# A two-block transformer kernel: small transfers change their queue, and two 8 KB slots join the weight ring

## The chip, the cores and the metric

One core of one Trainium2 chip. The metric is device time in microseconds of one execution, lower is better; each median is over several runs.

## What is computed

Two transformer blocks on 256 tokens of width 1024, in float32. Cut to what matters here:

```python
def first_block(x, ...):
    proj = modulate(rms_norm(x, g1), shift1, scale1) @ w_in   # width 5120
    o_sb, o_mb = stick_breaking_attention(...), moba_attention(..., rel_bias)
    x = x + gate1 * (merge(o_sb, o_mb) @ w_out)
    h2 = modulate(rms_norm(x, g2), shift2, scale2)
    # 64 experts, D=1024 -> 256 -> 1024; each token takes the best 8 of 4 groups of experts
    x = x + gate2 * (sum_e weight[t, e] * swiglu(h2, gate_e, up_e, down_e) + swiglu(h2, shared))
    return rms_norm(x, final_g)

def second_block(x, mem, ...):
    x = x + mix(short_conv, latent_attention) @ w_mix_out
    x = x + memory_cross_attention(x, mem)
    x = x + expert_choice_moe(x)          # 16 experts, D=1024 -> 1024 -> 1024; each takes its best 32 tokens
    return rms_norm(x, g)
```

The kernel reads every expert's weights once: 3 MiB for each of the 64, 12 MiB for each of the 16.

## The kernel before

**Weights.** Every weight comes in pieces of 128 x 2048 float32, 1 MiB, 8 KB on each partition. `load(src)` takes the next slot of a ring of such slots (`lanes`, a deque of slot numbers), issues the transfer on SyncE (L104) and returns the tile. The ring is changed by hand along the program: `add_lanes` appends slots that some other tile has given up, `drop_lanes` takes them back, `next_lanes` puts one at the front. It begins with ten slots (L293), five of which leave at L390. A load waits until the last reader of its slot is done. SyncE issues in order, so a load that waits holds up those behind it.

**Stages.** First the memory's keys (`memk`), the modulation (`ada`), the projections and the two attentions of block one, mostly as three float32r passes (`SP.feat`, L220) after a split of the weights on ScalarE and VectorE (L213, L214). Then routing (L755 to L898), then the first mixture, then block two's convolution, attention and memory attention, then the second mixture (L1600 to L1661).

**First mixture.** `layout` and the routing sort the experts by their number of tokens, and `_group_pairs` packs the order into 28 groups of 1, 2 or 4 experts, which share the 128 rows of a tile: eight groups of two, then four times (4, 1, 2, 2), then 4, 2, 4, 2. The first NF = 2 places are held by experts 0 and 1 whatever the routing says: `first_c` and `first_r` add 1000 x (NF - e) to their counts. So their six pieces are loaded ahead of the routing (`fixed`, L655), and group 0 uses them. All others wait for the sorted list `idx`: `Group.load` reads an expert's number into a register and issues its pieces (`eload`, L908): the halves of gate and up first, then down.

TensorE's order is written out by hand (L1055 to L1111): for each group `gate_up` (L999), parts of the `combine` of the group before (L1032, L1033) and of the `gather` for the next (L935, L936), filling work from `pieces()` (the memory's values L709, the shared expert L685 and L725), then `down` (L1023). `nxt.load()` stands at the start of each group, so one group's weights are requested while the group before is computed. Ring during this stage: eight slots at first; slots 2 and 10 join when the values are done, 11 and 7 after the shared expert's up half, 16 at its end. Slot 15 is lent for one load of group 1 (L1054, L1071).

**Order on the other engines** is made by a scheduler from the program order and its own estimates of time; only TensorE in the first mixture is fixed.

**Second mixture.** Per expert eight gate/up pieces (L1565) and four down pieces (L1634), all through `load` on SyncE; the ring has 16 slots there (17 after L1577).

**Small transfers.** Thirteen transfers are issued by GpSimd: `t5` (tables of the relative bias, L352), its product `rel` to DRAM (L358) and back as the skewed `relU` (L360), the router's weights, bias and limits (L399 to L403), three of six 1 MiB pieces that `park` brings for the filling work (L649; the other three are SyncE's), `wov` to DRAM (L898, read only by the branch for experts with too many tokens, L1116), the rotary tables (L1195, L1197) and the second router's weights (L1455). GpSimd's transfers need an area of SBUF for their descriptors.

Of the kernel before, what the change touches and what calls it, by code (L numbers as in the profile page):

```python
# [21 lines left out]
P = 128  # L22
# [8 lines left out]


N_EXP = 64
NF, N1, N2 = 2, 4, 34
CAP1, CAP2, CAP4 = 128, 64, 32


def _group_pairs():
    s = [(NF + i, 1) for i in range(N1)]
    p = [(0, NF)] + [(NF + N1 + 2 * i, 2) for i in range(N2 // 2)]  # L40
    q = [(NF + N1 + N2 + 4 * i, 4) for i in range((N_EXP - NF - N1 - N2) // 4)]
    out = []
    while s or p or q:
        g = []
        for lst in (p, p) if len(out) < 4 or not q or (len(out) % 2 and len(p) - 2 >= len(q) - len(s)) else (q, s or p):
            if lst:
                g.append(lst.pop(0))
        if g:
            out.append(g)
    return out  # L50
# [4 lines left out]
def body(tc, I, out):  # L55
    nc = tc.nc
# [34 lines left out]
    def add_lanes(*ids):  # L91
        lanes.extend(ids)

    def next_lanes(*ids):
        lanes.extendleft(reversed(ids))

    def drop_lanes(*ids):
        for i in ids:
            lanes.remove(i)

    def load(src):
        w = ring_tile()
        w = w[:, :src.shape[-1]]
        nc.sync.dma_start(w, src)  # L104
        return w
# [50 lines left out]
    def token_sums(acc):  # L156

        ps = bank("t")
        for b in range(2):
            nc.tensor.matmul(ps[:, b:b + 1], acc[:, b * P:(b + 1) * P], ones[:, :1], start=True, stop=True)  # L160
        return ps[:, :2]
# [128 lines left out]
    pa = b1.enter_context(tc.tile_pool(name="pa", bufs=1))  # L290
    open_banks(b1, "b1", d=2, s=3, t=2, a=1)
    SP = Split(14, 15, 16)
    add_lanes(17, 18, 19, 20, 21, 5, 6, 10, 12, 13)  # L293

# [15 lines left out]
    def ada_cols(ps, pair0, n):  # L312
        row = pa.tile([P, 512], F32, name="ada_row", tag="t512", bufs=3)
        nc.vector.tensor_copy(row, ps)
        pc = bank("t").rearrange("p (a u) -> p a u", a=4)
        for a in range(4):
            nc.tensor.matmul(pc[:, a, :n], row[:, a * P:(a + 1) * P], ident32[:, :n], start=True, stop=True)
        flat_mod = mod.rearrange("p g k -> p (g k)")[:, 4 * pair0:4 * (pair0 + n)]
        nc.vector.tensor_add(flat_mod.rearrange("p (u a) -> p a u", a=4), pc[:, :, :n],
                             col("b_ada", 48)[:, 4 * pair0:4 * (pair0 + n)].rearrange("p (u a) -> p a u", a=4))  # L320
# [8 lines left out]
    def memk(i):  # L329
        SP.feat(None, hm_hi, hm_lo, 256, KD,  # L330
                lambda j, ps: nc.vector.tensor_mul(mem_k[:, 2 * i:2 * i + 2], ps,
                                                   rm[:, None, :].to_broadcast([P, 2, T])), loaded=wk[i])
# [11 lines left out]
    for k in range(KD):  # L344
# [4 lines left out]
    nc.gpsimd.affine_select(out=flip, in_=flip, pattern=[[1, P]], base=1 - P, channel_multiplier=1,  # L349
                            compare_op=ALU.is_equal, fill=0.0)  # L350
    t5 = big(9, [32, 776], F32, "t5")
    nc.gpsimd.dma_start(t5, I["t5"])  # L352
    ps_r = bank("t")
    nc.tensor.matmul(ps_r[:8, :384], t5[:, :8], t5[:, 8:392], start=True, stop=True)
    rel = pa.tile([8, 384], F32, name="rel", tag="t512", bufs=3)
    nc.vector.tensor_add(rel, ps_r[:8, :384], t5[:8, 392:])
    rel_d = dram.tile([8, 384], F32, name="rel_d")
    nc.gpsimd.dma_start(rel_d, rel)  # L358
    relU = big(3, [P, 8, 256], F32, "relU")
    nc.gpsimd.dma_start(relU, bass.AP(tensor=rel_d.tensor, offset=rel_d.offset,  # L360
                                      ap=[[1, P], [384, 8], [1, 256]]))
    memk(0)
    r1 = rstd_of(pa, xT, KD, D)
    xr = big(7, [P, KD, T], F32, "xr")
# [3 lines left out]
    for i in range(4):  # L368
        mm = ada(ps_a, i, i == 0, i == 3, i)
        if i < 3:  # L370
            wk.append(load(I["w_mem_kv"][i + 1]))
            if i < 2:
                memk(i + 1)
    ada_cols(ps_a, 0, 4)
    memk(2)
    memk(3)
# [19 lines left out]
    nc.gpsimd.tensor_mul(fgfg, fg, fg)  # L396

    wr = pa.tile([P, KD, 64], F32, name="wr")
    nc.gpsimd.dma_start(wr, I["w_router"])  # L399
    rbias = const.tile([P, 64], F32, name="rbias")  # L400
    nc.gpsimd.dma_start(rbias, I["router_bias"].to_broadcast([P, 64]))
    caprow = const.tile([1, 64], F32, name="caprow")
    nc.gpsimd.dma_start(caprow, I["caprow"])  # L403


    qk = {}
# [235 lines left out]
    extra = deque([I["w_mem_kv"][4 + c] for c in range(4)] + [I["w_up_sh"], I["w_down_sh"]])  # L642
    parked = deque()

    def park(eng=nc.gpsimd):
        if extra:
            w = big(wide[0], [P, 2048], F32, "wx")
            wide.rotate(-1)
            eng.dma_start(w, extra.popleft())  # L649
            parked.append(w)  # L650

    for _ in range(2):
        park(nc.sync)
    shg = load(I["w_gate_sh"])
    fixed = [load(I["w_gu"][e, u]) for u in range(2) for e in range(NF)] + [load(I["w_down_e"][e]) for e in range(NF)]  # L655
    park(nc.sync)
    r2 = rsqrt_of(pa, token_sums(acc), D, sig_last[0])
    r2c = const.tile([P, 2], F32, name="r2c")
    nc.gpsimd.tensor_copy(r2c, r2)
# [235 lines left out]
    wov = selT  # L895
    nc.vector.scalar_tensor_tensor(wov, rkT, capc, wT, op0=ALU.is_ge, op1=ALU.mult)
    wov_d = dram.tile([64, T], F32, name="wov_d")
    nc.gpsimd.dma_start(wov_d, wov)  # L898


    xgs, yys = deque((3, 4)), deque((14, 15))
# [37 lines left out]
    class Group:  # L939
# [8 lines left out]

        def load(self):
            self.regs, self.gu, self.wd = [], [], []  # L950
            if self.i0 == 0:
                self.gu = [fixed[NF * half:NF * half + NF] for half in range(2)]
                self.wd = fixed[2 * NF:]
                return
            first = []
            for j in range(self.n):
                with tc.issue_after(issued[-8]) if len(issued) >= 8 else nullcontext():
                    self.regs.append(nc.sync.value_load(idx[0:1, self.i0 + j:self.i0 + j + 1], min_val=0, max_val=63))
                first.append(eload(I["w_gu"], self.regs[j], 0))
            self.gu = [first, [eload(I["w_gu"], r, 1) for r in self.regs]]  # L960
            self.wd = [eload(I["w_down_e"], r, None) for r in self.regs]
# [89 lines left out]
    with tc.issue_after(slots(0).ins):  # L1051
        for a in range(2):
            shared_act(0, a, gate[a])
    next_lanes(15)  # L1054
    with tc.manual_schedule(engines={mybir.EngineType.PE}):  # L1055
        gr[0].load()
        for q in range(4):
            gather(0, q)
            piece()
        gr[0].place()  # L1060
        piece()
        gr[0].weigh()
        for i, u in enumerate(gr):
            prev, nxt = gr[i - 1] if i else None, gr[i + 1] if i + 1 < len(gr) else None
            pn = u.pi + 1
            if u.g == 0 and pn < len(GROUP_PAIRS):
                slots(pn)
            if nxt:
                nxt.load()
                if i == 0:  # L1070
                    drop_lanes(15)  # L1071
            if nxt is gr[-1]:
                piece(1000)
                drop_lanes(1, 2, 7, 10, 11, 12, 13, 20)
                early = [load(I["w_in2"][c]) for c in (12, 13, 0, 8, 4)]
                fl = nc.values_load(flagi[0:1, 0:1], min_val=0, max_val=1)
            if nxt is None:
                for k in range(KD):
                    nc.vector.scalar_tensor_tensor(xT[:, k], y1[:, k], mod[:, 5, k:k + 1], xT[:, k],
                                                   op0=ALU.mult, op1=ALU.add)  # L1080
            u.gate_up()

            gs_ = []
            if pn < len(GROUP_PAIRS):
                half = len(GROUP_PAIRS[u.pi]) > 1
                gs_ = [2 * u.g, 2 * u.g + 1] if half else [0, 1, 2, 3]
            fills = FILL[u.n]

            def c(q):
                if prev:  # L1090
                    prev.combine(q, last=nxt is None)
            c(0)
            if gs_:
                gather(pn, gs_[0])
            piece(fills)
            c(1)
            u.flip()
            if nxt:
                nxt.place()
            c(2)  # L1100
            if gs_:
                gather(pn, gs_[1])
            piece(fills)
            c(3)
            if nxt:
                nxt.weigh()
            for q in gs_[2:]:
                gather(pn, q)
            u.down()
        for q in range(4):  # L1110
            gr[-1].combine(q, last=True)  # L1111
# [80 lines left out]
            nc.vector.scalar_tensor_tensor(acc2, sq[:, k], fgfg[:, k:k + 1], acc2, op0=ALU.mult, op1=ALU.add)  # L1192
    SP.feat(None, h_hi, h_lo, 256, KD, lambda j, ps: held.append(ps), tag="s", loaded=early[1])
    cos2 = pb.tile([P, T], F32, name="cos2")
    nc.gpsimd.dma_start(cos2, I["cos"])  # L1195
    sin2 = pb.tile([P, T], F32, name="sin2")
    nc.gpsimd.dma_start(sin2, I["sin"])  # L1197
    r1 = rsqrt_of(pb, token_sums(acc), D)
    m2 = pb.tile([P, 2], F32, name="m2")
    nc.vector.tensor_mul(m2, r1, r1)  # L1200
# [251 lines left out]
    wr2 = pb.tile([P, KD, 32], F32, name="wr2")  # L1452
    nc.gpsimd.memset(wr2, 0.0)
    wr2s = pb.tile([P, KD, E2], F32, name="wr2s")
    nc.gpsimd.dma_start(wr2s, I["w_router2"])  # L1455
    nc.gpsimd.tensor_copy(wr2[:, :, :E2], wr2s)
    ident4 = pb.tile([P, E2], F32, name="ident4")
    nc.vector.tensor_add(ident4, ident2[:, :E2], ident2[:, 32:32 + E2])
# [111 lines left out]
    first = []  # L1570
# [144 lines left out]
def layout(inp):  # L1715
# [52 lines left out]
    e = np.arange(64)  # L1768
    first = np.where(e < NF, 1000 * (NF - e), 0).astype(np.float32)
# [9 lines left out]
    o["w_gate_sh"] = _chunks(g["w_gate_sh"][0], KD, 256, True)[0]  # L1779
    o["w_up_sh"] = _chunks(g["w_up_sh"][0], KD, 256, True)[0]  # L1780
    o["w_down_sh"] = _chunks(_perm_out(g["w_down_sh"][0]), 2, D, False)[0]
    e = np.arange(P)
    first = np.where(e < NF, 1000 * (NF - e), 0).astype(np.float32)
    addv("first_c", first[:, None])
    addv("first_r", np.broadcast_to(first[:64], (P, 64)))
    o["vec"] = np.ascontiguousarray(np.concatenate(cols, axis=1))
# [29 lines left out]
```

## Time and profile before

| | |
|---|---|
| median of 3 runs | 1656.02 us (1654.62 to 1658.31) |
| profiled execution, its own time | 1653.91 us |
| its span, first to last instruction | 1651.9 us |
| TensorE busy / VectorE / ScalarE / GpSimd | 87% / 37% / 26% / 7% |
| moved | 524.76 MB, mean 318 GB/s |
| granted TensorE clock, mean | 0.927 |

The span is 2.0 us shorter than the execution's own time, which in turn is 2.1 us below the median. Busy shares are averages over stages with different limits, so the stages are read one by one: the slices show where the DMA engines run at their highest rate, the windows and timelines what TensorE and SyncE's queue wait for there.

### The profile page before, as it was taken

The numbers are of one execution on the slowest core, as the hardware profiler recorded it, in microseconds if no ns is written. First come the engines' busy times: TensorE is split into PE (matmuls) and PEld (weight loads), VectorE is DVE, ScalarE is ACT, GpSimd is POOL, SyncE is SP. The second block draws the span as 40 slices with busy tenths as digits, with TensorE's granted clock in tenths as the row PEclk, the third lists the DMA queues.
The fourth block names the chain that finished last, engine by engine and source line by source line (L and its number), as shares of the span: only waits on it lengthen the run. The fifth ranks groups of instructions, "written<-read, shape, count | busy, mean of one in ns | idle before, by whom it ended". The sixth has DMA issues, their size and how long they took to land. (4 is left out here: it accounts for less than half of the span.)

```text
span 1651.9 us, 23990 instructions
## 1 busy us (share of the span) xinstructions
PE 1430.5 (87%) x9780; PEld 903.4 (55%) x9780; DVE 614.6 (37%) x1111; ACT 433.1 (26%) x756; POOL 116.1 (7%) x168
## 2 busy tenths in 40 slices
PE   6999999899999999999788999999787666676674
PEld 5768898645544455544368889998432122121121
DVE  6433655432323233333376566675321011111122
ACT  4453544211111111112155535454210000000001
POOL 3010201200000000000021110011100000000001
PEclk9999999999999999999889999999897778868777
DMA  9685744488998999999943335575399999999995
GB/s 383 268 306 219 294 170 160 157 347 360 385 394 355 415 388 421 410 420 420 421 159 131 125 136 205 197 279 224 136 418 421 421 421 421 421 421 421 421 421 216
DMA packets 72896, 524.76 MB, mean 318 GB/s; under 512 B 8201, under 2 KB 8337, under 8 KB 9297
## 3 DMA queue, kind: packets, MB, share of 16 engines
q1 hardware_dynamic: 71712, 518.22, 78.3%
q0 software_dynamic: 1072, 5.00, 0.8%
q8 instruction: 77, 1.26, 0.3%
q14 instruction: 35, 0.28, 0.0%
HBM read 521.01 MB, written 2.17 MB: 317 GB/s over the span
## 5 line engine op out<-in xcount | busy, mean ns | idle before, releaser
L214 DVE TENSOR_TENSOR whl<-w,whl 128x1024 fp32r<-128x1024 f32 x156 | 195.7, 1260 | 145.4 <-ACT whl L213 144.7
L220 PE MATMUL ps_d<-h_hi,whl 128*128 128x256 f32 x1216 | 227.4, 286 | 0.0
L999 PE MATMUL ps_u<-w,xg 128*64 128x512 f32 (+2 forms) x1024 | 209.2, 604 | 7.8 <-DMA w<-in_w_gu 7.8
L213 ACT CAST whl<-w 128x1024 fp32r<-128x1024 f32 x156 | 162.6, 1048 | 165.8 <-PE ps_d L220 138.4
L220 PEld LDWEIGHTS ps_d<-h_hi,whl 128*128 128x128 f32 x1216 | 190.2, 190 | 6.0 <-issue 3.2
L220 PE MATMUL ps_d<-h_lo,whl 128*128 128x256 f32 x608 | 172.3, 283 | 0.0
L999 PEld LDWEIGHTS ps_u<-w,xg 128*64 128x64 f32 (+2 forms) x1024 | 66.7, 131 | 146.5 <-issue 126.8
L1565 PE MATMUL ps_u<-w,xgb 128*32 128x512 f32 x512 | 97.9, 844 | 52.8 <-DMA w<-in_w_gu 52.8
L220 PEld LDWEIGHTS ps_d<-h_lo,whl 128*128 128x128 f32 x608 | 115.1, 189 | 1.1 <-issue 0.9
L1565 PE MATMUL ps_u<-w,xga 128*32 128x512 f32 x512 | 92.9, 694 | 20.0 <-DMA w<-in_w_gu 20.0
L1634 PE MATMUL ps_y<-w,aT 128*32 128x256 f32 x1024 | 84.1, 474 | 27.7 <-DMA w<-in_w_down 23.6
L1023 PE MATMUL ps_y<-w,aT 128*64 128x512 f32 (+2 forms) x512 | 104.6, 607 | 0.0
L1032 PE MATMUL ps_c<-S,yy 128*128 128x256 f32 x224 | 73.8, 351 | 20.6 <-DVE y L1042 13.3
L1622 DVE SCALAR_TENSOR_TENSOR act<-ps_u,wsl,sl 128x256 f32<-128x256 f32 x16 | 7.7, 484 | 217.3 <-ACT sl L1612 217.3
L1042 DVE TENSOR_TENSOR y<-ps_c,y 128x512 f32<-128x512 f32 x100 | 68.6, 686 | 53.5 <-PE ps_c L1033 53.5
L1005 DVE SCALAR_TENSOR_TENSOR act<-ps_u,wsl,sl 128x256 f32<-128x256 f32 x28 | 13.6, 484 | 189.7 <-ACT sl L1003 189.7
L1565 PEld LDWEIGHTS ps_u<-w,xgb 128*32 128x32 f32 x512 | 12.7, 125 | 126.9 <-DMA w<-in_w_gu 121.9
L1612 ACT ACTIVATE sl<-ps_u 128x256 f32<-128x256 f32 x16 | 6.1, 383 | 280.6 <-PE ps_u L1565 280.6
L1634 PEld LDWEIGHTS ps_y<-w,aT 128*32 128x32 f32 x1024 | 33.8, 131 | 75.0 <-DMA w<-in_w_down 43.8
L1032 PEld LDWEIGHTS ps_c<-S,yy 128*128 128x128 f32 x224 | 42.6, 190 | 49.8 <-issue 21.2
L213 ACT CAST yy<-ps_y 128x512 fp32r<-128x512 f32 x56 | 32.8, 585 | 115.4 <-PE ps_y L1023 115.4
L1003 ACT ACTIVATE sl<-ps_u 128x256 f32<-128x256 f32 x28 | 10.8, 384 | 198.8 <-PE ps_u L999 198.8
(506 smaller groups left out, 2316.5 us busy)
## 6 DMA issues: line engine op xcount, KB each, us to landing
w<-in_w_gu SPq DMA_DIRECT2D x256, 1024.0 KB, 15.7
w<-in_w_down_e SPq DMA_DIRECT2D x64, 1024.0 KB, 11.5
w<-in_w_down SPq DMA_DIRECT2D x64, 1024.0 KB, 19.9
w<-in_w_in SPq DMA_DIRECT2D x42, 1024.0 KB, 6.0
w<-in_w_ada SPq DMA_DIRECT2D x24, 1024.0 KB, 7.7
w<-in_w_mem_kv SPq DMA_DIRECT2D x4, 1024.0 KB, 19.6
w<-in_w_out SPq DMA_DIRECT2D x4, 1024.0 KB, 4.8
w<-in_w_conv_out SPq DMA_DIRECT2D x4, 1024.0 KB, 4.8
```

Of the source, the lines that this page charges most:

```text
L213: nc.scalar.copy(hi, src)
L214: eng.tensor_sub(lo, src, hi.bitcast(F32))
L220: nc.tensor.matmul(region, l, r, start=(start and u == 0), stop=(stop and u == 2), skip_group_check=True)
L999: nc.tensor.matmul(pg[cap * j:cap * (j + 1)], xg[:, 4 * half + k, cap * j:cap * (j + 1)], ws[j][:, k], start=(half == 0 and k == 0), stop= ...
L1003: silu[:] = [nc.scalar.activation(sl, pg[:, :256], AF.Silu)]
L1005: nc.vector.scalar_tensor_tensor(self.act, pg[:, 256:], self.wsl, sl, op0=ALU.mult, op1=ALU.mult)
L1023: nc.tensor.matmul(py[cap * j:cap * (j + 1)], self.aT[:, f, cap * j:cap * (j + 1)], wd[j][:, f, h * 512:(h + 1) * 512], start=(f == 0), st ...
L1032: nc.tensor.matmul(ps[:, a], self.yy[:, 0, k * P:(k + 1) * P], self.S, start=True, stop=False)
L1042: nc.vector.tensor_add(y1[:, 2 * q:2 * q + 2], ps, y1[:, 2 * q:2 * q + 2])
L1565: mm = nc.tensor.matmul(pg[32 * j:32 * j + 32], xg[k][:, 32 * e:32 * e + 32], w[:, 512 * j:512 * j + 512], start=(k == 0), stop=(k == KD - ...
L1622: nc.vector.scalar_tensor_tensor(act, pg[:, 256:], wsl[:, e % 4, e // 4:e // 4 + 1], sl, op0=ALU.mult, op1=ALU.mult)
L1634: nc.tensor.matmul(py[32 * j:32 * j + 32, :256], aT[:, f, 32 * v:32 * v + 32], w[:, f, 256 * j:256 * j + 256], start=(v == 0 and f == 0), ...
```

## The change

The area for GpSimd's descriptors shrinks to 256 bytes a partition, and slots 22 and 23 join the ring at its start. All thirteen transfers leave GpSimd: ten go to ScalarE's queue (`t5`, `wr`, `rbias`, `caprow`, three `park`, `cos2`, `sin2`, `wr2s`), three to SyncE's (`rel_d`, `relU`, `wov_d`), the latter at later places of the program. NF becomes 4, the fixed experts are 0, 1, 62 and 63, and the number of sorted pairs falls from 34 to 32 experts; the 28 groups keep their sizes and order. Group 0 (experts 0 and 1) and group 1 (62 and 63) now need no routing. Their twelve pieces: ten ring loads, of which one waits for the shared gate's slot, and two in the borrowed slots 15 and 4.

```diff
-NF, N1, N2 = 2, 4, 34
+FIRST = (0, 1, 62, 63)
+NF, N1, N2 = len(FIRST), 4, 32
...
-    p = [(0, NF)] + [(NF + N1 + 2 * i, 2) for i in range(N2 // 2)]
+    p = [(2 * i, 2) for i in range(NF // 2)] + [(NF + N1 + 2 * i, 2) for i in range(N2 // 2)]
...
-    add_lanes(17, 18, 19, 20, 21, 5, 6, 10, 12, 13)
+    add_lanes(17, 18, 19, 20, 21, 22, 23, 5, 6, 10, 12, 13)
...
-    nc.gpsimd.dma_start(t5, I["t5"])
+    nc.scalar.dma_start(t5, I["t5"])
...
-    nc.gpsimd.dma_start(rel_d, rel)
...
-    nc.gpsimd.dma_start(relU, bass.AP(tensor=rel_d.tensor, offset=rel_d.offset,
-                                      ap=[[1, P], [384, 8], [1, 256]]))
...
+        if i == 0:
+            nc.sync.dma_start(rel_d, rel)
+        if i == 2:
+            nc.sync.dma_start(relU, bass.AP(tensor=rel_d.tensor, offset=rel_d.offset,
+                                            ap=[[1, P], [384, 8], [1, 256]]))
...
-    nc.gpsimd.dma_start(wr, I["w_router"])
+    nc.scalar.dma_start(wr, I["w_router"])
...
-    nc.gpsimd.dma_start(rbias, I["router_bias"].to_broadcast([P, 64]))
+    nc.scalar.dma_start(rbias, I["router_bias"].to_broadcast([P, 64]))
...
-    nc.gpsimd.dma_start(caprow, I["caprow"])
+    nc.scalar.dma_start(caprow, I["caprow"])
...
-    def park(eng=nc.gpsimd):
+    def park(eng=nc.scalar):
...
-    fixed = [load(I["w_gu"][e, u]) for u in range(2) for e in range(NF)] + [load(I["w_down_e"][e]) for e in range(NF)]
+    fixed = {}
+    def fixed_load(what, e):
+        src = I["w_down_e"][e] if what == 2 else I["w_gu"][e, what]
+        fixed[what, e] = load(src)
+    for e in FIRST[:2]:
+        fixed_load(1, e)
+    for e in FIRST[:2]:
+        fixed_load(2, e)
+    for what in range(3):
+        for e in FIRST[2:]:
+            if what < 2 or e == FIRST[2]:
+                fixed_load(what, e)
     park(nc.sync)
+    next_lanes(15, 4)
+    for e in FIRST[:2]:
+        fixed_load(0, e)
+    drop_lanes(15, 4)
+    fixed_load(2, FIRST[3])
...
-    nc.gpsimd.dma_start(wov_d, wov)
...
-            if self.i0 == 0:
-                self.gu = [fixed[NF * half:NF * half + NF] for half in range(2)]
-                self.wd = fixed[2 * NF:]
+            if self.i0 < NF:
+                es = FIRST[self.i0:self.i0 + self.n]
+                self.gu = [[fixed[half, e] for e in es] for half in range(2)]
+                self.wd = [fixed[2, e] for e in es]
                 return
...
-    next_lanes(15)
...
-                if i == 0:
-                    drop_lanes(15)
+                if i == 2:
+                    nc.sync.dma_start(wov_d, wov)
...
-    nc.gpsimd.dma_start(cos2, I["cos"])
+    nc.scalar.dma_start(cos2, I["cos"])
...
-    nc.gpsimd.dma_start(sin2, I["sin"])
+    nc.scalar.dma_start(sin2, I["sin"])
...
-    nc.gpsimd.dma_start(wr2s, I["w_router2"])
+    nc.scalar.dma_start(wr2s, I["w_router2"])
...
-    first = np.where(e < NF, 1000 * (NF - e), 0).astype(np.float32)
+    first = np.zeros(P, np.float32)
+    first[list(FIRST)] = 1000 * (NF - np.arange(NF))
...
-    nc = bacc.Bacc("TRN2", target_bir_lowering=False, num_devices=1)
+    nc = bacc.Bacc("TRN2", target_bir_lowering=False, num_devices=1, dynamic_dma_scratch_size=256)
```

## Rows read from the trace of the kernel before

**Rows 1.** The page's 40 slices of 41.3 us: gigabytes per second moved.
```profile
GB/s 383 268 306 219 294 170 160 157 347 360 385 394 355 415 388 421 410 420 420 421 159 131 125 136 205 197 279 224 136 418 421 421 421 421 421 421 421 421 421 216
```

**Rows 2.** Windows by stage: engine busy, clock, DMA share, GB/s last.
```profile
317.00:575.00 258.00, 243.63 (x1356) 130.31 (x1356) 74.18 (x163) 45.84 (x91) 1.64 (x3) 1.00 0.92 369
...
575.00:825.00 250.00, 231.91 (x1364) 118.25 (x1360) 82.04 (x174) 42.55 (x81) 0.00 (x0) 0.98 1.00 412
...
1125.00:1190.00 65.00, 54.03 (x351) 43.43 (x349) 29.82 (x62) 23.27 (x50) 12.96 (x19) 0.92 0.45 175
...
1190.00:1632.00 442.00, 319.23 (x2340) 97.69 (x2340) 64.78 (x116) 21.98 (x52) 0.00 (x0) 0.80 1.01 418
```

**Rows 3.** The chain that ended last, its end: start, length, what.
```profile
1612.49 19.98 DMA w<-in_w_down
...
1632.52 1.11 PE ps_y L1634 x16
```

**Rows 4.** Timeline of TensorE, L999 in the first mixture: start, length, count.
```profile
457.98 4.49 PE L999 MATMUL ps_u<-w,xg 128*32 128x512 f32 x36
...
465.49 3.62 PE L999 MATMUL ps_u<-w,xg 128*32 128x512 f32 x26 [1.50 <-DMA w<-in_w_gu]
...
534.16 4.49 PE L999 MATMUL ps_u<-w,xg 128*32 128x512 f32 x36
...
541.85 3.62 PE L999 MATMUL ps_u<-w,xg 128*32 128x512 f32 x26 [1.43 <-DMA w<-in_w_gu]
...
610.57 7.07 PE L999 MATMUL ps_u<-w,xg 128*32 128x512 f32 x64
...
784.71 4.48 PE L999 MATMUL ps_u<-w,xg 128*32 128x512 f32 x34
...
794.88 5.67 PE L999 MATMUL ps_u<-w,xg 128*32 128x512 f32 x26 [0.58 <-DMA w<-in_w_gu]
```

**Rows 5.** Timeline of SyncE and TensorE around the first group of four.
```profile
439.79 7.20 SPq L908 DMA_DIRECT2D w<-in_w_gu  x5
...
447.23 0.33 SPq L908 DMA_DIRECT2D w<-in_w_gu  x1
...
454.39 3.65 PE L1023 MATMUL ps_y<-w,aT 128*64 128x512 f32 x16
...
458.07 0.91 SPq L908 DMA_DIRECT2D w<-in_w_gu  x2
```

**Rows 6.** Timeline of SyncE's issues where the second mixture begins.
```profile
1173.98 0.33 SPq L104 DMA_DIRECT2D w<-in_w_gu  x1
...
1187.64 0.33 SPq L104 DMA_DIRECT2D w<-in_w_gu  x1
```

**Rows 7.** Waits of TensorE from 64 to 130 us.
```profile
PE ps_d L220 <- ACT whl L213: 1.9, 1, 1.9
```

**Rows 8.** Start of the program: SyncE's issues, and landing of memT.
```profile
1.24 0.42 SPq L324 DMA_DIRECT2D hm<-in_memT  x1
...
6.21 0.33 SPq L104 DMA_DIRECT2D w<-in_w_mem_kv  x1
...
hm<-in_memT SPq DMA_DIRECT2D x1, 1024.0 KB, 4.9
```

**Rows 9.** GpSimd's and SyncE's transfers: issue, landing, and who reads relU.
```profile
22.70 0.55 POOL L358 DMA_DIRECT2D rel_d<-rel  x1 [2.96 <-DVE rel L356]
...
relU<-rel_d POOLq DMA_DIRECT2D x1, 1024.0 KB, 12.6
...
L380 PE MATMUL ps_t<-relU,flip x8: 591/592/697, 58.0 to 62.4; 128*128 128x512 f32 x8
...
w<-in_w_down SPq DMA_DIRECT2D x64, 1024.0 KB, 19.9
```

**Rows 10.** Tile wx: what one trigger takes its queue (ns min, median, max).
```profile
L649 SPq DMA_DIRECT2D wx<-in_w_mem_kv x3: 328/328/328, 258.9 to 281.5; - x3
...
L649 POOL DMA_DIRECT2D wx<-in_w_mem_kv x1: 579/579/579, 345.8 to 345.8; - x1
```

More of the change, by code (lines that the diff above doesn't have):

```diff
@@ L1781, in layout @@
     o["w_down_sh"] = _chunks(_perm_out(g["w_down_sh"][0]), 2, D, False)[0]
-    e = np.arange(P)
-    first = np.where(e < NF, 1000 * (NF - e), 0).astype(np.float32)
+    first = np.zeros(P, np.float32)
+    first[list(FIRST)] = 1000 * (NF - np.arange(NF))
     addv("first_c", first[:, None])
```

## The prediction, made before the result was known

> **What bounds the kernel now.** The slices come first, since two loaded resources take turns here. Counted from 1, the rate stands at 420 to 421 GB/s in slices 18 to 20 and at 421 from 31 to 39 [rows 1]; nothing in the row is higher, so there the DMA engines are full, and 1 MiB (1.0486 MB) costs 1.0486 / 0.421 = 2.49 us. Elsewhere they are half idle. The windows then say what TensorE does in these stretches [rows 2]: from 317 to 575 us it is busy for 243.6 of 258 us at full clock with a DMA share of 0.92 (TensorE is the bound), from 575 to 825 us both are full, and from 1190 to 1632 us it is busy for only 319 of 442 us with a DMA share of 1.01 (DMA is the bound). The chain that ended last agrees: its last transfer lands at 1632.5 us and TensorE works on it at once [rows 3]. So a load that comes earlier is worth something at two places: in the second mixture, always, and in the first, where TensorE visibly waits for weights.
>
> Those waits are read from the `gate_up` of the groups of four. One that waits for nothing takes 7.07 us (610.57). The first takes 465.49 + 3.62 - 457.98 = 11.13 us, the second 541.85 + 3.62 - 534.16 = 11.31 us, the last 794.88 + 5.67 - 784.71 = 15.84 us [rows 4]. They lose 4.06, 4.24 and 8.77 us.
>
> **The change part by part.**
>
> *Two more slots, first mixture.* For the first group of four, six of eight gate/up pieces are issued from 439.79 to 447.56 us, the last two only at 458.07 us, when the group before has ended its `down` (454.39 + 3.65 = 458.04) [rows 5]. The ring has eight slots, two are held by that group's `down` weights, and the four need eight. With ten slots the two go out at 447.6 us. They then land behind what is queued, eight pieces from 439.8 us: at the latest 439.8 + 2.2 + 8 x 2.49 = 461.9 us, where 2.2 us is what the 4.9 us of one transfer into an idle queue leave beside 2.49 [rows 8]. They are the second half of the sum, not read before 458.0 + 3.5 us, so the wait falls from 4.06 us to 0.4 at most. The second group of four has the same ring and the same pattern. Gain 8.3 us, bounds 7.5 and 8.3.
>
> What is late next is the last group of four. From 575 us DMA is full, so what it lacks at 784.7 us depends on how far ahead the loads were when DMA became the bound. TensorE reaches that point 8.3 us earlier, and the loads with it, since until then they are issued when TensorE frees a slot; two more slots hold 2 x 2.49 = 5.0 us more. The last wait shrinks from 8.77 to 3.8 us. Gain 5.0 us; below, nothing, if the queue loses in gaps what it had gained; above, all of 8.8.
>
> *Four experts instead of two.* No row shows TensorE waiting for group 1's weights: there is no DMA wait between 284 and 400 us, and `gate_up` of group 1 is undisturbed. Six pieces fewer after the routing are 15 us of DMA, but at 317 to 575 us DMA is not the bound and the ring is full anyway. The six extra pieces move into slices 6 to 8, which run at 157 to 170 GB/s [rows 1]; their slots come from the two new ones and from 15 and 4, which are lent until the first group has read them. I cost this part at nothing in both directions; what covers it is that idle DMA.
>
> *Two more slots, second mixture.* The loads run ahead until 1173.98 us, when the ring is full; the next one is issued at 1187.64 us, when the first expert frees a slot [rows 6]. From there DMA never pauses. Two more slots let two more pieces be moved before, in a window with a DMA share of 0.45 [rows 2]. Gain 2 x 2.49 = 5.0 us. I see no bound far from it: the ring is empty of waits after, and TensorE has 123 us to spare.
>
> *Two more slots, block one.* One wait of 1.9 us for a weight split that was late by its load [rows 7]. Gain 1.0 us, between 0 and 1.9.
>
> *Transfers on ScalarE and SyncE.* A trigger costs SyncE 0.33 us and GpSimd 0.58 us [rows 10]; no row has one on ScalarE. Ten of them are 3.3 to 5.8 us of ScalarE's time. Most lie where ScalarE is idle (in the first mixture it is busy for 46 of 258 us [rows 2], and `t5` waits for nothing), so below is 0. But ScalarE is in order, and in the start its casts are ahead of TensorE. How long a trigger there can wait is shown by SyncE: its tenth transfer goes out at 6.21 us, just after its second has landed (1.24 + 4.9 = 6.14) [rows 8], though its slot is free; and landing takes 19.9 us with the queue full, eight times 2.49 [rows 9]. Eight transfers are in flight and a ninth waits for the oldest. If ScalarE's triggers count among these eight, `wr`, `rbias` and `caprow`, issued at some 12 us amid the first loads, hold it till the oldest three have landed: three steps of 2.49 us, 7.5 us. I take 2 us for all ten, near the lower end, because TensorE's start waits for ScalarE only in part; bounds 0 and 7.5 + 1.5.
>
> *The rel tables on SyncE.* `rel_d` is issued at 22.70 us as soon as `rel` exists, and `relU` is read at 58.0 us [rows 9]. On SyncE both stand behind weights: at worst two landings of 19.9 us, 22.7 + 39.8 = 62.5 us, 4.5 us too late. But `relU` cannot be issued before `rel_d` has landed, and SyncE issues nothing meanwhile, so the queue is nearly empty for the second: 22.7 + 19.9 + 12.6 = 55.2 us, 2.8 us early. Cost 0, bound 4.5. The Trainium skill's "DMA: Bandwidth & Descriptors", section "Queues, rings and completion order", speaks against this edit: each DMA engine works off a queue's ring in order and takes turns between the queues' rows, so that a small transfer of GpSimd's slips past weights and one of SyncE's does not. By that rule the worst case of 4.5 us is the likelier one for `rel_d`'s half; no row before shows a small transfer on SyncE behind weights. `wov_d` goes to SyncE at a time when it waits for slots, and its reader is not run: 0.
>
> *Sorting.* The branch for overfull experts doesn't run before. With the reference's routing experts 0, 1, 62 and 63 have 46, 13, 11 and 13 tokens (limit 64), of the others the largest has 75 (128), the fifth 61 (64) and the thirty-seventh 26 (32): it doesn't run after either.
>
> Sum: -8.3 - 5.0 - 5.0 - 1.0 + 2.0 = -17.3 us. From the profiled execution's 1653.9 that gives 1636.6; the median shown is 2.1 us higher, so 1638.7, and I say 1639 us.
>
> **Rivals.** (a) *ScalarE is held in the start* at the upper bound, 9 us instead of 2: -10, 1646 us. For it: the eight in flight. Against: the scheduler may place these triggers before the queue fills. (b) *The first mixture gains nothing*, because its DMA share of 0.92 leaves little: the pieces moved earlier delay others. Then 5.0 + 1.0 - 2.0 = 4 us remain, 1652 us. Against: the two late pieces were late by a slot, not by the queue [rows 5]. (c) *Slower*: `park`'s three triggers sit on ScalarE's queue within the first mixture, in front of the copies and activations that TensorE waits for. If each waits for the oldest of eight loads, up to 19.9 us [rows 9], 3 x 19.9 = 60 us at most stand against the gain; it decides from 17.3 / 3 = 5.8 us each. With 11 us each the time would be 1672 us. Against: until 575 us the queue is not full, so the oldest has landed. (d) *All DMA waits of the first mixture go*: 3.8 us more, and no cost on ScalarE, 1633 us. (e) *It does not do what it says*: the scheduler reorders so that the new slots stay unused, 1656 us.
>
> **How the numbers follow.** Forecast 0.60 (its own range 1634 to 1643), (a) 0.12, (b) 0.10, (c) 0.08, (d) 0.07, (e) 0.03. The forecast, (a), (d) and half of (b) make about 0.84, so the range is 1630 to 1651. A change of 0.2%, 3.3 us, is about what can be told from none. Faster: forecast, (a), (d) and most of (b), 0.87; same: the rest of (b) and half of (e), 0.05; slower 0.08.
>
> **What the profile after would show.** The first two groups of four with 7.1 us of `gate_up` and eight gate/up issues before the `down` of the group before has ended; the last one with some 4 us of waiting; eighteen loads of the second mixture before its first expert frees a slot, and its last landing about 17 us earlier; `rel_d` landing in 10 to 20 us; ScalarE's triggers without long gaps ahead of them. I am wrong if ScalarE shows waits of several microseconds for a load in front of a trigger, if TensorE waits at the first routed group (2, at about 351 us), or if `relU` lands after 58 us.

## The result, and the profile after

| | before | after |
|---|---|---|
| median | 1655.32 us (4 runs, 1651.38 to 1658.31) | 1636.22 us (4 runs, 1633.32 to 1637.62) |
| profiled execution, its own time | 1653.91 us | 1637.62 us |
| its span | 1651.9 us | 1635.8 us |

The ratio is 0.9884, 95% interval 0.9857 to 0.991: faster by 1.2%, 19.2 us by the ratio (15 to 24). The forecast was 1639 us, 1630 to 1651. The two profiled executions differ by 16.3 us, since that of before lies 1.4 us below its median and that of after, the longest of its four, 1.4 us above.

The slices of after, gigabytes per second:

```profile
GB/s 327 340 348 211 297 167 223 68 376 342 383 390 403 416 418 421 415 420 420 420 162 143 115 143 203 196 284 217 140 420 421 421 421 420 421 421 421 421 421 215
```

Against [rows 1], the first slice moves less (327 for 383), the pieces of the four fixed experts stand in slice 7 (223 for 160) and leave slice 8 nearly empty (68 for 157), and in the first mixture slices 9, 13 and 15 move more (376 for 347, 403 for 355, 418 for 388) and slice 10 less (342 for 360). The full rate is the same 421.

The same windows as in [rows 2] (busy time of TensorE first, then of its weight loads and the other engines; last the granted clock, DMA share, GB/s):

```profile
317.00:575.00 258.00, 247.76 (x1399) 133.48 (x1400) 75.85 (x166) 46.59 (x92) 0.00 (x0) 1.00 0.91 372
575.00:825.00 250.00, 228.35 (x1351) 117.12 (x1350) 88.45 (x185) 46.15 (x84) 0.00 (x0) 0.98 1.01 418
1125.00:1190.00 65.00, 54.17 (x350) 38.09 (x348) 25.92 (x56) 22.74 (x48) 12.00 (x17) 0.92 0.57 222
1190.00:1632.00 442.00, 310.56 (x2311) 96.31 (x2311) 71.89 (x130) 22.38 (x56) 6.37 (x9) 0.78 0.97 404
```

TensorE is busy for 247.76 of the first 258 us instead of 243.63, and ahead of the second mixture the DMA share is 0.57 instead of 0.45. The 0.97 in the last window is no slower DMA: the loads are through before it ends.

The timeline of TensorE, `gate_up` (L999 is now L1021) of the first, second and last group of four, and of the last group of two:

```profile
458.11 7.07 PE L1021 MATMUL ps_u<-w,xg 128*32 128x512 f32 x64
...
530.18 7.07 PE L1021 MATMUL ps_u<-w,xg 128*32 128x512 f32 x64
...
776.46 4.67 PE L1021 MATMUL ps_u<-w,xg 128*32 128x512 f32 x38
782.58 3.62 PE L1021 MATMUL ps_u<-w,xg 128*32 128x512 f32 x26 [1.45 <-DMA w<-in_w_gu]
...
796.10 1.07 PE L1021 MATMUL ps_u<-w,xg 128*64 128x512 f32 x2
797.54 3.65 PE L1021 MATMUL ps_u<-w,xg 128*64 128x512 f32 x16 [0.37 <-DMA w<-in_w_gu]
802.47 3.65 PE L1021 MATMUL ps_u<-w,xg 128*64 128x512 f32 x14 [1.27 <-DMA w<-in_w_gu]
```

The first two groups of four wait for nothing (11.13 and 11.31 us in [rows 4]). The last takes 782.58 + 3.62 - 776.46 = 9.74 us instead of 15.84. The next lines say why the first one waits no more: SyncE's issues for it, and the `down` of the group before it.

```profile
429.38 18.30 SPq L929 DMA_DIRECT2D w<-in_w_gu  x8
...
454.52 3.65 PE L1045 MATMUL ps_y<-w,aT 128*64 128x512 f32 x16
...
458.20 3.89 SPq L929 DMA_DIRECT2D w<-in_w_down_e  x3
```

All eight gate/up pieces are issued by 447.7 us; in [rows 5] two of them waited for the end of that `down`, to 458.07 us. Now it is pieces of the `down` half that wait for a slot, which are needed later.

SyncE ahead of the second mixture, and the end of the chain that ended last:

```profile
1076.34 45.54 SPq L105 DMA_DIRECT2D w<-in_w_gu  x9
1121.98 12.86 SPq L105 DMA_DIRECT2D w<-in_w_down  x4
1134.89 43.85 SPq L105 DMA_DIRECT2D w<-in_w_gu  x7
...
1163.61 0.33 SPq L105 DMA_DIRECT2D w<-in_w_gu  x1
1176.29 2.45 SPq L105 DMA_DIRECT2D w<-in_w_gu  x2
```

```profile
1596.62 19.84 DMA w<-in_w_down
1620.04 1.88 DVE xT L1675 x3
```

Of the 20 pieces in the first three lines the last two, at 1176.29 us, are the first that wait for the first expert: eighteen go out before it frees a slot (sixteen up to 1173.98 us in [rows 6]). The last load is issued at 1596.62 us, 15.9 us earlier than in [rows 3].

The start of the program shows what the prediction had not seen: SyncE's issues, its longest wait there, `relU`'s landing, and its reader (four views).

```profile
6.98 0.33 SPq L105 DMA_DIRECT2D w<-in_w_mem_kv  x1
23.23 0.35 SPq L373 DMA_DIRECT2D rel_d<-rel  x1
...
26.75 0.40 SPq L375 DMA_DIRECT2D relU<-rel_d  x1
```

```profile
SPq L373 <- DVE acc L154: 15.9, 1, 15.9
```

```profile
relU<-rel_d SPq DMA_DIRECT2D x1, 1024.0 KB, 18.9
```

```profile
L383 PE MATMUL ps_t<-relU,flip x8: 592/592/697, 59.4 to 62.7; 128*128 128x512 f32 x8
```

`rel_d` stands in SyncE's queue in front of six loads and `relU`, but its data are ready only at about 23 us (VectorE writes `rel` from 22.66 to 23.21 us; the profile puts the wait down to VectorE's next instruction): SyncE issues nothing for 16 us. In the first 25 us the DMA share falls from 0.94 to 0.71, and in the first 60 us TensorE is busy for 43.9 instead of 45.2 us. Yet the routing ends (`idx`) at 301.0 us, against 301.2 before.

`park`'s three triggers on ScalarE take 0.33 to 0.36 us and have no wait ahead of them (these two lines are typical):

```profile
345.73 0.36 ACTq L652 DMA_DIRECT2D wx<-in_w_mem_kv  x1
...
417.04 0.33 ACTq L652 DMA_DIRECT2D wx<-in_w_up_sh  x1
```

### The profile page after: what moved, and what is told of

It reads as the page before. It is cut to its first block, busy times and chain, and to the rows that moved or that the text cites. A ratio compares the mean times of both kernels' runs of the same rounds, so it can differ in the third digit from the quotient of the medians.

```text
span 1635.8 us, 23949 instructions
## 1 busy us (share of the span) xinstructions
PE 1419.8 (87%) x9780; PEld 903.9 (55%) x9780; DVE 615.4 (38%) x1111; ACT 431.8 (26%) x756; POOL 101.8 (6%) x155
## 3 DMA queue, kind: packets, MB, share of 16 engines
q8 instruction: 77, 1.26, 0.3%
## 5 line engine op out<-in xcount | busy, mean ns | idle before, releaser
L1021 PE MATMUL ps_u<-w,xg 128*64 128x512 f32 (+2 forms) x1024 | 200.5, 594 | 3.1 <-DMA w<-in_w_gu 3.1
L1021 PEld LDWEIGHTS ps_u<-w,xg 128*64 128x64 f32 (+2 forms) x1024 | 64.9, 130 | 134.9 <-issue 127.2
L1586 PE MATMUL ps_u<-w,xga 128*32 128x512 f32 x512 | 95.7, 708 | 19.1 <-DMA w<-in_w_gu 19.0
L1054 PE MATMUL ps_c<-S,yy 128*128 128x256 f32 x224 | 74.0, 352 | 20.9 <-DVE y L1064 13.3
L1027 DVE SCALAR_TENSOR_TENSOR act<-ps_u,wsl,sl 128x256 f32<-128x256 f32 x28 | 13.6, 484 | 176.5 <-ACT sl L1025 176.5
L1633 ACT ACTIVATE sl<-ps_u 128x256 f32<-128x256 f32 x16 | 6.1, 383 | 275.2 <-PE ps_u L1586 275.1
L215 DVE TENSOR_TENSOR yy<-ps_y,yy 128x512 fp32r<-128x512 f32 x56 | 38.7, 691 | 57.7 <-ACT yy L214 57.7
## 6 DMA issues: line engine op xcount, KB each, us to landing
w<-in_w_gu SPq DMA_DIRECT2D x256, 1024.0 KB, 16.3
```

The source lines that it names most:

```text
L215: eng.tensor_sub(lo, src, hi.bitcast(F32))
L1021: nc.tensor.matmul(pg[cap * j:cap * (j + 1)], xg[:, 4 * half + k, cap * j:cap * (j + 1)], ws[j][:, k], start=(half == 0 and k == 0), stop= ...
L1027: nc.vector.scalar_tensor_tensor(self.act, pg[:, 256:], self.wsl, sl, op0=ALU.mult, op1=ALU.mult)
L1054: nc.tensor.matmul(ps[:, a], self.yy[:, 0, k * P:(k + 1) * P], self.S, start=True, stop=False)
L1586: mm = nc.tensor.matmul(pg[32 * j:32 * j + 32], xg[k][:, 32 * e:32 * e + 32], w[:, 512 * j:512 * j + 512], start=(k == 0), stop=(k == KD - ...
```

## The experiments

Four points divide each profile into stages: the first `gate_up` of the first mixture, the first matmul of block two (`ps_s`), the first gather of the second mixture (`ps_g<-G`), and the issue of the last load. They come from the timeline of TensorE and the end of the chain; before: 317.44, 840.34, 1181.96 and 1612.49 us. The last column is the ratio to the runs of before that ran beside it on the same chip.

| kernel | median us | start | first mixture | block two | second mixture | ratio, 95% interval |
|---|---|---|---|---|---|---|
| before | 1655.3 | 317.4 | 522.9 | 341.6 | 430.5 | |
| after | 1636.2 | 317.6 | 510.0 | 344.0 | 425.0 | 0.9884, 0.9857 to 0.9910 |
| after, again | 1637.6 | 318.2 | 509.3 | 342.2 | 425.6 | 0.9895, 0.9882 to 0.9908 |
| moves_only | 1653.8 | 316.7 | 521.6 | 342.3 | 430.8 | 0.9995, 0.9981 to 1.0009 |
| ring_only | 1637.0 | 318.1 | 509.4 | 342.2 | 426.2 | 0.9880, 0.9861 to 0.9899 |
| four_temp | 1653.4 | 317.6 | 521.9 | 341.8 | 430.1 | 0.9992, 0.9980 to 1.0005 |
| second_only | 1650.2 | 317.9 | 522.7 | 342.9 | 426.2 | 0.9959, 0.9942 to 0.9975 |
| first_only | 1641.4 | 316.4 | 509.5 | 342.0 | 430.0 | 0.9920, 0.9907 to 0.9933 |
| one_slot | 1645.0 | 318.1 | 516.0 | 342.4 | 428.1 | 0.9941, 0.9929 to 0.9953 |
| rel_early | 1636.4 | 317.4 | 509.6 | 343.7 | 426.4 | 0.9881, 0.9867 to 0.9896 |
| act_late | 1634.7 | 315.9 | 509.3 | 343.8 | 426.2 | 0.9876, 0.9860 to 0.9893 |
| fours_sooner | 1634.0 | 317.0 | 507.5 | 341.8 | 425.7 | 0.9876, 0.9853 to 0.9898 |
| fours_sooner_two_fixed | 1634.6 | 319.7 | 506.1 | 342.1 | 425.9 | 0.9878, 0.9856 to 0.9900 |
| fours_sooner_rel_early | 1632.7 | 314.7 | 508.0 | 342.4 | 426.1 | 0.9867, 0.9851 to 0.9884 |

The theory: the two slots bring the whole gain, in two separate places, and neither the experts nor the queues count. The rivals: the six pieces that need no routing bring a part, or the moved transfers do (or take some).

**The parts by themselves.** `moves_only` is the kernel before with the thirteen transfers moved and the descriptors' area shrunk as in the change, and nothing else. `ring_only` adds the slots to it:

```diff
-    add_lanes(17, 18, 19, 20, 21, 5, 6, 10, 12, 13)
+    add_lanes(17, 18, 19, 20, 21, 22, 23, 5, 6, 10, 12, 13)
```

`four_temp` is the changed kernel in which the slots serve only the loads ahead of the routing:

```diff
-    add_lanes(17, 18, 19, 20, 21, 22, 23, 5, 6, 10, 12, 13)
+    add_lanes(17, 18, 19, 20, 21, 5, 6, 10, 12, 13)
...
+    add_lanes(22, 23)
     shg = load(I["w_gate_sh"])
...
     fixed_load(2, FIRST[3])
+    drop_lanes(22, 23)
```

> Only the thirteen transfers leave GpSimd's queue; two fixed experts, no new slots. Theory (the slots bring the gain, the moves cost next to nothing, since the start's loss is made good before the routing ends): 1655 to 1657 us, first gate_up of four at 11.1 us as before, SyncE held some 16 us by rel_d at the start. Rival (the moves themselves are a gain or a cost): 1650 or less, or 1660 or more.

> The moves and slots 22 and 23, but only experts 0 and 1 fixed, loaded as before the change. Theory (slots alone): 1636 us within 3, first two groups of four at 7.1 us. Rival (the six pieces, 15 us of transfers, that need not follow the routing bring a part): 1641 to 1650 us, with TensorE waiting for weights in groups 1 to 3 or with the fours as slow as before.

> Four fixed experts, but slots 22 and 23 serve only their loads ahead of the routing and then leave the ring for good. Theory (experts bring nothing without the slots): 1655 us within 2, first two groups of four at 11 us again. Rival (the six pieces bring it): 1640 to 1650 us, the last group of four with less than 13 us of gate_up.

All three came out as the theory has it, `moves_only` 1.2 us below its range. The slots without the experts give the whole gain (1637.0 us), the experts without the slots none (1653.4 us beside 1653.8 with the moves alone). In `four_temp` the first group of four waits as in [rows 4], 465.44 + 3.62 - 458.02 = 11.04 us:

```profile
458.02 4.49 PE L1023 MATMUL ps_u<-w,xg 128*32 128x512 f32 x36
462.96 1.04 PE L1023 MATMUL ps_u<-w,xg 128*32 128x512 f32 x2 [0.46 <-DMA w<-in_w_gu]
465.44 3.62 PE L1023 MATMUL ps_u<-w,xg 128*32 128x512 f32 x26 [1.44 <-DMA w<-in_w_gu]
```

**The slots, place by place.** `second_only` is `moves_only` whose slots join in block two; `first_only` is the changed kernel whose slots leave at the end of the first mixture:

```diff
-    add_lanes(2, 8, 9, 10, 5)
+    add_lanes(2, 8, 9, 10, 5, 22, 23)
```

```diff
-                drop_lanes(1, 2, 7, 10, 11, 12, 13, 20)
+                drop_lanes(1, 2, 7, 10, 11, 12, 13, 20, 22, 23)
```

> The moves, two fixed experts, and slots 22 and 23 join the ring only in block two, ahead of the second mixture's loads. Theory: 2 x 2.49 = 5.0 us below the kernel that has the moves alone, so 1650 to 1651 us, eighteen loads before the first expert frees a slot. Rival (in the second mixture the gain is what was earned earlier and only carried through): no more than 1 us, 1654 to 1656 us.

> The changed kernel, but slots 22 and 23 leave the ring at the end of the first mixture. Theory (two separate gains): the last group of four and the start of block two as in the changed kernel (829 us), then sixteen loads instead of eighteen before the first expert of the second mixture frees a slot, and 5 us are lost: 1641 us. If the 1.4 us that block two gave back come from the longer ring there, they return and it is 1640. Rival (the second mixture's lead is inherited from the first): 1636 to 1637 us.

> The changed kernel once more, beside the three others of this set, so that small differences are read on one chip: 1636 us within 2.

The two gains are separate. With slots in the second mixture alone it takes 426.2 us instead of 430.8 (4.6 less), with slots in the first alone the second is back at 430.0. What block two seemed to give back in the trace of after (344.0 against 341.6 us; the expectation says 1.4, since it starts one row later in after) is no effect of the ring: the same kernel profiled again has 342.2.

**The dose.** `one_slot` is `ring_only` with slot 22 alone.

> Dose: the moves and one new slot (22) instead of two, two fixed experts. Theory: the second mixture gains one piece, 2.5 us; of the two pieces that were late for the first groups of four one goes out early, the other is still late but is the last one read, so most of 4 us each stays lost: between 1645 and 1649 us. Rival (one slot is enough, the second is spare): 1639 us or less.

Its first group of four:

```profile
458.59 4.49 PE L1000 MATMUL ps_u<-w,xg 128*32 128x512 f32 x38
463.49 3.62 PE L1000 MATMUL ps_u<-w,xg 128*32 128x512 f32 x26 [0.41 <-DMA w<-in_w_gu]
```

463.49 + 3.62 - 458.59 = 8.52 us: 1.45 us are lost, where no new slot loses 4 and two lose none, so each slot brings the late piece forward by about one transfer (2.49 us) until none is late. The expectation had "most of 4 us each stays lost"; it is a third (the second group of four takes 537.16 + 3.62 - 532.11 = 8.67 us). The last group of four takes 789.13 + 3.62 - 779.96 = 12.79 us, between 15.84 with no new slot and 9.74 with two. The second mixture takes 428.1 us, 2.4 less than before; with both slots it is 4 to 5.5 less. The smaller loss fits a time of 1645.0 us, at the lower edge of the expected range.

**SyncE's hold at the start.** `rel_early` computes `rel` (L352 to L357 of after) ahead of the split of the memory, so that `rel_d` need not wait for VectorE.

> The changed kernel with the small product rel computed at the start of the program, ahead of the memory's split on VectorE, so that SyncE need not wait 15.9 us for it. Theory (the hold costs nothing in the end, as the routing ended at 301.0 us against 301.2 before): DMA share of the first 25 us back above 0.9, the routing's end within 1 us of 301.0, time 1635 to 1636.5 us. Rival (the hold costs what TensorE lost in the first 60 us, 1.0 + 0.3 us, or more): the routing ends by 299.5 us, time 1634.5 us or less.

Window, issue, and the wait of `relU`'s trigger in `rel_early`:

```profile
0.00:25.00 25.00, 10.48 (x57) 8.84 (x58) 14.69 (x39) 14.40 (x32) 7.80 (x24) 1.00 0.90 357
...
7.83 0.35 SPq L373 DMA_DIRECT2D rel_d<-rel  x1
...
SPq L375 <- DMA rel_d<-rel: 2.2, 1, 2.2
```

The hold is gone and the share is 0.90 (0.94 before the change). `rel_d` now travels behind weights: `relU`, which waits for it, goes out at 21.16 us, 13.3 us after it. TensorE reads `relU` at 57.9 us, 1.5 us earlier than after; but `idx` comes at 300.9 us, against 301.0 and 301.5 in the two profiles of after, and the medians (1636.4 against 1637.6) are not apart. With the same edit it came at 299.5 and 299.6 us in the two kernels below. Whether the hold costs 1 us or nothing can't be told: the first `gate_up` starts anywhere from 314.7 to 319.7 us in the table, wider than what is asked.

**ScalarE's triggers amid the loads.** `act_late` is `rel_early` with

```diff
-    nc.scalar.dma_start(wr, I["w_router"])
+    with tc.issue_after(last.ins):
+        nc.scalar.dma_start(wr, I["w_router"])
```

and the same for `rbias` and `caprow` (`last` is the last square of the memory).

> The kernel with the early rel, and the triggers of wr, rbias and caprow moved on ScalarE behind its squares of xT, to about 20 us, where SyncE's queue is full. Theory (rival (a) of the prediction as a mechanism: what spared ScalarE was that its triggers came at 0.8 to 4 us, ahead of the loads): if the eight in flight count transfers of both queues, ScalarE stands some 2.5 us at each trigger, 7.5 us in all, the casts of w_mem_kv behind it come later, and the time is up to 7 us longer, 1637 to 1643 us. Rival (a trigger of ScalarE doesn't count SyncE's loads): no gap above 1 us ahead of these triggers, 1635 to 1637.5 us.

ScalarE's timeline, and then SyncE's largest waits up to 60 us, in `act_late`:

```profile
18.85 0.36 ACTq L403 DMA_DIRECT2D wr<-in_w_router  x1
19.24 0.45 ACTq L406 DMA_DIRECT2D rbias<-in_router_bias  x1
19.72 0.54 ACTq L409 DMA_DIRECT2D caprow<-in_caprow  x1
20.30 1.04 ACT L214 CAST whl<-w 128x1024 fp32r<-128x1024 f32 x1 [1.04 <-issue]
```

```profile
SPq L105 <- DMA wr<-in_w_router: 7.4, 1, 7.4
...
SPq L105 <- DMA rbias<-in_router_bias: 3.4, 1, 3.4
```

The theory failed: ScalarE does not wait. The three triggers cost it 1.35 us together, with the queue full (the DMA share from 12 to 25 us is 1.01), and 1634.7 us is 0.3 below what the rival gave. But the theory's premise seems to hold from the other side: SyncE waits 7.4 and 3.4 us for the landing of ScalarE's small transfers before it issues loads that have nothing to do with them, as it would if the transfers of both queues count together. The first of these waits ends as `wr` lands (18.85 + 7.5 = 26.35 us). No cost of it is seen: the DMA share is 1.02 from 19.0 to 26.4 us and 0.94 from there to 30.2 us, and the time is no longer than `rel_early`'s.

**A further version: the groups of four sooner.** In after the DMA share is 0.85 from 317 to 450 us and full at the end of the stage, where `gate_up` still waits. `fours_sooner` changes one number in `_group_pairs`, so that the groups of four begin after two pairs of twos and are spread to the end; `fours_sooner_two_fixed` does the same in `ring_only`, `fours_sooner_rel_early` in `rel_early`:

```diff
-        for lst in (p, p) if len(out) < 4 or not q or (len(out) % 2 and len(p) - 2 >= len(q) - len(s)) else (q, s or p):
+        for lst in (p, p) if len(out) < 2 or not q or (len(out) % 2 and len(p) - 2 >= len(q) - len(s)) else (q, s or p):
```

> The changed kernel with another order of its 28 groups: the groups of four begin after the first two pairs of twos, not after four, and are spread evenly up to the end (the order of the groups is free). In the changed kernel DMA is busy for 0.85 of the time from 317 to 450 us and full from 575 us on, where gate_up still waits for weights by some 5 to 7 us in all. Theory (the bytes come too late in the stage): these waits shrink, 1630 to 1634 us. Rival (with ten slots the early groups of four wait for slots, 12 pieces against 10): 1637 us or more.

> The same order of groups in the kernel with the two slots and only two fixed experts. Theory (the six pieces that need no routing bring something once DMA is loaded early in the stage, since 15 us of transfers are then missing ahead of the first groups of four): slower than the same order with four fixed experts by 2 us or more. Rival (they bring nothing there either): within 1.5 us of it.

> The order of groups that spreads the groups of four, together with the early rel. Theory (the start's hold is made good before the routing ends, so that the early rel adds nothing): 1632.5 to 1635 us, as the order alone. Rival (it gives the 1.3 us that TensorE lacked in the first 60 us): 1632 us or less.

TensorE's wait for gate and up weights from 576 to 830 us, in after and then in `fours_sooner`:

```profile
PE ps_u L1021 <- DMA w<-in_w_gu: 3.1, 3, 1.4
```

```profile
PE ps_u L1021 <- DMA w<-in_w_gu: 0.5, 1, 0.5
```

`fours_sooner` is at the upper edge of what was expected. TensorE hardly waits for these weights any more: 0.5, 0 and 0.7 us in the three kernels. The 3.1 us of after are high for the old order, which has 1.1 to 1.3 us in the five other profiles with both slots in the first mixture. The first mixture takes 506.1 to 508.0 us in the three kernels, against 509.3 to 510.0 in the six profiles that have both slots there and the old order. Two fixed experts are as good as four here too: the theory of `fours_sooner_two_fixed`, 2 us slower, failed.

What the order brings in time is not clear of noise. The three medians lie below the two of after, the lowest, 1632.7 us, by 3.6 and 5.0 us (and 22 us below before). But `act_late`, with the old order, has the same ratio as `fours_sooner` (0.9876), and the interval of the lowest (0.9851 to 0.9884) touches that of after's second set (0.9882 to 0.9908) and overlaps that of the first. The nearest pair on one chip is `fours_sooner_rel_early` and `act_late`, 1632.7 against 1634.7 us.

## Why the prediction was right, and where it was off

The time came from the terms that the prediction named, and two small terms of opposite sign were both too large; that they partly cancelled is luck.

- *First two groups of four, -8.3 us:* right. The group after the second four starts at 550.27 us instead of 558.49, 8.2 us earlier, with the eight issues where they were promised. `four_temp`, `one_slot` and `ring_only` show that it is the number of slots: 4, 1.45 and 0 us of waiting for none, one and two. (In the bound on what was left, 4.9 us less 2.49 is 2.4 and not 2.2 us; that moves it from 0.4 to 0.6 us.)
- *Last group of four, -5.0 us:* right in size. Its `gate_up` takes 9.74 us instead of 15.84, 6.1 less: it loses 2.67 us now, not 3.8. But of the 8.77 us lost before, about 2.9 were slow matmuls and not waiting. After two waits for weights (0.71 and 1.45 us) the granted clock was 0.50, that is 1.2 instead of 2.4 GHz, from 792.4 to 799 us; two matmuls took 1.91 instead of 1.04 us there, and the last 26 took 5.67 instead of 3.62 [rows 4]. After has 1.00 there. The first two of these lines are of before, the last two of `four_temp`, which has the old ring and a clock of 1.00:

```profile
789.89 1.04 PE L999 MATMUL ps_u<-w,xg 128*32 128x512 f32 x2 [0.71 <-DMA w<-in_w_gu]
792.38 1.91 PE L999 MATMUL ps_u<-w,xg 128*32 128x512 f32 x2 [1.45 <-DMA w<-in_w_gu]
...
784.25 4.48 PE L1023 MATMUL ps_u<-w,xg 128*32 128x512 f32 x34
...
794.65 3.62 PE L1023 MATMUL ps_u<-w,xg 128*32 128x512 f32 x26 [1.45 <-DMA w<-in_w_gu]
```

`four_temp` takes 794.65 + 3.62 - 784.25 = 14.02 us, and the five other profiles with both slots and the old order 9.17 to 9.28. So the slots' own part is 4.3 to 4.9 us by these profiles; the rest of the 6.1 goes with the clock. Why it fell in before, `moves_only` and `second_only` and not in `four_temp`, no run shows. What the last group of two adds can't be told: its `gate_up` takes 10.02 us in after and 9.10 in before, but 7.7 to 8.3 in those five profiles and 7.1 to 9.3 in the three others with the old ring there. Over the whole first mixture the table has -12.9 us (-13.6 in the second profile) where the prediction had -13.3.
- *Four experts, 0:* right, and shown three times (`ring_only`, `four_temp`, `fours_sooner_two_fixed`).
- *Second mixture, -5.0 us:* right: eighteen pieces, and 425.0 to 426.4 us in the nine profiles that have both slots there, against 430.0 to 430.8 in the four that have neither: 3.6 to 5.8 us.
- *Block one, -1.0 us:* the wait shrank from 1.9 to 1.1 us, and nothing of it is seen at the first `gate_up`, which came 0.1 us later. The term was too large.
- *ScalarE, +2.0 us:* too large; this is the term that was mis-sized. `moves_only` has the ratio 0.9995, -0.8 us (-3.1 to +1.5) for all thirteen moves. The triggers cost 0.33 to 0.54 us each and waited for nothing. The upper bound and rivals (a) and (c) rested on one sentence, that ScalarE's triggers might wait for the oldest of eight transfers. They don't in any profile. In after `wr`, `rbias` and `caprow` went out at 1.26 to 3.86 us, not at some 12 us; `act_late` put them amid the loads, and it was SyncE that waited.
- *The rel tables, 0:* the cost was right within what can be seen, the path wrong. `relU` landed at 45.7 us, not 55, and `rel_d` within 3.5 us (`relU` goes out at 26.75), not in 10 to 20. The prediction had the time at which `rel` is ready, and asked when the transfers would land behind weights; it didn't ask what stands behind a trigger that waits for `rel`. SyncE and its loads did, for 15.9 us, and because of it the queue was empty when `rel_d` went out. The row was there: GpSimd had waited for `rel` up to 22.70 us [rows 9], where no weight stood behind it. Behind weights `rel_d` does take 13.3 us (`rel_early`). By an estimate from that run's two landings the tables would be in time even so: 22.7 + 13.3 + 18.8 = 54.8 us, ahead of 58.0.

The Trainium skill's "DMA: Bandwidth & Descriptors", section "Queues, rings and completion order", has each DMA engine work off a queue's ring in order and take turns between the queues' rows; the prediction drew from it that a small transfer of GpSimd's slips past weights and one of SyncE's does not. The runs agree. The 12 KB of `rel_d` took 13.3 us in SyncE's queue behind weights (`rel_early`; the loads issued just before it took 13.3 to 14.3 us), and 5.0 us from GpSimd's queue in before, with a DMA share of 0.98. In `act_late` the 256 KB of `wr`, issued by ScalarE at 18.85 us, landed at 26.4 us, ahead of the load that SyncE had issued at 18.69 us, which landed at 30.5 us. `relU` tells little, since it is 1 MiB itself: 12.6 us from GpSimd's queue [rows 9], 18.9 us from SyncE's.

The rivals: (b) fell with the two groups of four, (c) and (a) with the triggers, (e) with the eighteen issues, and (d) needed the last group's wait to go, which the order of the groups does, not the slots. Without the two mis-sized terms the sum would have been -18.3 us; the median fell by 19.1 us, and by the ratios of the two sets 19.2 and 17.4.

## What to carry to other kernels

Where loads stall, ask of each whether it waits for the bus or for a place to land: a piece issued late because its slot was taken was worth here about one transfer time (2.4 to 2.6 us) per slot added, at each place where the ring was full, and the places added up. Loading more ahead of a decision brought nothing here, since the ring, not the decision, set when pieces went out. Before a transfer is moved onto an in-order queue, ask when its data are ready and what stands behind it there, not only how long it will travel.

## What was unexpected of the hardware

- Transfers of SyncE's and ScalarE's queues seem to share one count of transfers in flight: in `act_late` SyncE stood 7.4 us for `wr` (256 KB) and 3.4 us for `rbias` (32 KB), both issued by ScalarE; in `rel_early` it stood 3.5 us for `rbias`, and in after 1.0 us for `t5`. Whether the hardware or the program's semaphores make that limit, no run here tells.
- A trigger costs ScalarE 0.33 to 0.54 us with the engines full or not, about SyncE's 0.33 to 0.42 [rows 8, 10]; GpSimd's thirteen took 0.51 to 0.96 in before.
- A profile of the same kernel moves by 2 us within a stage in which nothing changed (block two: 344.0 and 342.2 us), and the start by 5 us over all kernels (314.7 to 319.7), though the medians agree within 1.4 us: a difference of one stage between two single profiles is worth no more than that.
